# The last chunk of two layers done tile by tile, third sums released sooner, and the parked residual stream cut into eight pieces

## The chip, the cores and the metric

The kernel runs on one core of a Trainium2 chip. The metric is the device time of one execution in microseconds (us), lower is better. The core has five engines that run side by side, each with its own instruction queue: TensorE (PE: matmuls, with a weight-load part PEld), VectorE (DVE), ScalarE (ACT), GpSimd (POOL) and SyncE (SP), which here only issues DMA transfers. Engines wait for each other through semaphores; transfers run on 16 DMA engines that all queues share.

## The reference

One encoder layer in fp32 over 256 positions of 2048 features. Three sub-layers follow each other; each normalises its input, multiplies it with weights, normalises the result and adds it to the residual stream h:

```python
hn = rms_norm(h, g_mix_pre)
u = hn @ w_in                                   # 2048 x 5120
attn, rec = attention(q, k, v), rglru(xr) * gelu(yg)
mixed = concat(rms_norm(attn), rms_norm(rec)) @ w_out      # 2048 x 2048
h = h + rms_norm(mixed, g_mix_post)
fn = rms_norm(h, g_ffn_pre)
ff = (silu(fn @ w_ffn_gate) * (fn @ w_ffn_up)) @ w_ffn_down  # 2048 x 5632 x 2048
h = h + rms_norm(ff, g_ffn_post)
gate = sigmoid(rms_norm(h, g_ple_pre) @ w_ple_gate)        # 2048 x 2048
h = h + rms_norm(gate * (p @ w_ple_proj), g_ple_post)      # p is 256 wide
```

What matters here are the two seams at which h gets its addition: no matmul of the next sub-layer can start until the last column of `mixed` (or of `ff`) is there, because the norm needs the sum of squares over all 2048 columns.

## The kernel before, in words

**Numbers.** A matmul in fp32 is made of three in a rounded format (fp32r): every operand is split into a high part (a cast on ACT) and the rest (a subtraction on DVE), and hi x hi, lo x hi and hi x lo are summed. A weight tile is 256 rows (two blocks of 128) by 512 columns, 512 KB: SP loads it into `wr`, ACT casts `wh` from it (L699), DVE subtracts `wl` (L715), and PE runs twelve matmuls with it: two blocks, two row tiles of 128 positions (`acc0`, `acc1`), three products (L753 to L755 in `products`).

**Chunks.** The output columns are taken 512 at a time. A chunk is such a quarter of 2048 columns, with its two accumulators `acc0` and `acc1`; its `post` runs when its last weight tile is done. The two tiles' matmuls alternate within each block, so both accumulators are finished almost together.

**The seam.** For the mixing layer the post of a chunk is `Sub.chunk`: ACT sums the squares of each accumulator (`squares`, L1612), DVE multiplies it by the gain into `mg` (L1594). For the channel layer DVE first adds what earlier groups left (L1582). When all four chunks are done, `next_norm` adds up the squares (L1627), gets 1/rms (a root on ACT, L397, a reciprocal on DVE, L399) and updates h in place, in pieces of 256 columns per tile (L1652). Blocks of h are transposed by PE (L343) and split into `hT_hi` (ACT, L330) and `hT_lo` (DVE, L332) for the next sub-layer. The last quarter (blocks 12 to 15) is turned in another way: DVE transposes 32x32 pieces, small DMA moves (`mT<-mid`, L362) put them in place, and the split reads `mT`. While the seam lasts, PE does matmuls that don't depend on it: those of the embedding `p @ w_ple_proj` (`embedding(0)`, `embedding(1)`).

**Third sums.** Some pairs of blocks of the channel layer are multiplied by a scheme with seven products for eight. It needs sums of blocks of hT (`sums_of`: L866, L873, then a split on ACT L324 and DVE L326), one set for each pair, and sums of weights (`sum_stream`: L640, L642, L646), which wait for the sums of hT. The third set, `more_sums`, uses blocks 4 and 5 and a buffer that had held `mg`; it starts when every block of hT has been made (`for e in hF.ev`).

**Parking.** `spill_h` writes h (two tiles of 128x2048, 1 MB each) to device memory, so that its place can hold weights (`lower`, `third`) until it is read back at the end of the channel layer. It is planned at the end of `next_norm`, and waits for all blocks of hT.

**Order.** The kernel is written under a planner that simulates the engines' clocks as it emits instructions. Work for the engines is a set of generators (tasks); when an engine is free, the planner picks among the tasks that are ready by time and by a lateness that each carries (`-SOON` brings it forward by 2 us, `LATE` puts it back). The order in which it emits is the order of each queue, and nothing overtakes in a queue.

## Time and profile before

| | |
|---|---|
| Median of 3 runs | 1139.5 us (1138.98 to 1141.05) |
| Profiled execution | 1141.41 us, span 1139.6 |
| PE busy | 1129.5 us, 99% of the span |
| DVE busy | 962.8 us, 84% |
| ACT busy | 741.3 us, 65% |
| POOL busy | 154.8 us, 14% |
| Mean DMA traffic | 237 GB/s |

All times in the profile's rows are us from the start of the span. A row of a timeline gives start, busy time, engine, line of the kernel, operation, output and inputs, and in brackets how long the engine had been idle before and what ended that. `x4` folds four equal instructions in a row. Durations of neighbours overlap a little, so the distance between starts is the better price. A row of waits gives total, number and longest. A row of stretches gives the stretch, its length, the busy time and count of PE, PEld, DVE, ACT and POOL, the granted clock of PE, the DMA share and GB/s. A row of transfers ends with the size of one and its median time from issue to landing. The mixing layer's seam lies around 340 to 362 us, the third sums around 380 to 396, the channel layer's seam around 1030 to 1052.

### The profile page before, as it was taken

The numbers are of one execution on the slowest core, as the hardware profiler recorded it, in microseconds if no ns is written. First come the engines' busy times: TensorE is split into PE (matmuls) and PEld (weight loads), VectorE is DVE, ScalarE is ACT, GpSimd is POOL, SyncE is SP. The second block draws the span as 40 slices with busy tenths as digits, with TensorE's granted clock in tenths as the row PEclk, the third lists the DMA queues.
The fourth block names the chain that finished last, engine by engine and source line by source line (L and its number), as shares of the span: only waits on it lengthen the run. The fifth ranks groups of instructions, "written<-read, shape, count | busy, mean of one in ns | idle before, by whom it ended". The sixth has DMA issues, their size and how long they took to land.

```text
span 1139.6 us, 15226 instructions
## 1 busy us (share of the span) xinstructions
PE 1129.5 (99%) x5140; PEld 937.4 (82%) x5140; DVE 962.8 (84%) x1250; ACT 741.3 (65%) x994; POOL 154.8 (14%) x245
## 2 busy tenths in 40 slices
PE   9999999999999999999999999999999999999997
PEld 7888888888888788888888888888888888888886
DVE  6768787788468899899998889999999988988886
ACT  6776788976447556566566656666656664676674
POOL 0000000000000032132011033141121223100200
PEclk9999999999999999999999999999999999999999
DMA  8867666565786977787887777887888787877863
GB/s 313 300 193 220 170 187 184 166 200 181 212 299 184 317 258 235 233 254 223 271 294 225 249 215 217 254 264 228 275 276 285 226 248 250 290 227 269 263 194 109
DMA packets 110687, 269.54 MB, mean 237 GB/s; under 512 B 36433, under 2 KB 42577, under 8 KB 109201
## 3 DMA queue, kind: packets, MB, share of 16 engines
q1 hardware_dynamic: 95568, 242.60, 63.6%
q0 software_dynamic: 14752, 25.84, 11.3%
q8 instruction: 40, 0.66, 0.2%
q14 instruction: 39, 0.31, 0.1%
q10 hardware_dynamic: 288, 0.14, 0.0%
HBM read 250.70 MB, written 9.44 MB: 228 GB/s over the span
## 4 chain that ended last, share of the span: by engine, by line
PE 96%; DVE 2%; ACT 1%; issue 0%; DMA 0%; SPq 0%; DVEq 0%; POOL 0%; ACTq 0%; POOLq 0%
PE acc L755 23%; PE acc L753 23%; PE acc L754 23%; PE acc L766 7%; PE acc L765 7%; PE acc L764 7%; PE tr L343 1%; DVE wl L715 1%; DMA sq<-ev 0%; PE half L2068 0%; PE acc L2068 0%; PE warm L2254 0%; PE pg L390 0%; PE pg L391 0%; PE pg L392 0%
## 5 line engine op out<-in xcount | busy, mean ns | idle before, releaser
L715 DVE TENSOR_TENSOR wl<-wr,wh 128x1024 fp32r<-128x1024 f32 (+1 forms) x295 | 352.7, 1209 | 78.8 <-ACT wh L699 74.6
L699 ACT CAST wh<-wr 128x1024 fp32r<-128x1024 f32 (+1 forms) x295 | 305.3, 1044 | 145.8 <-PE acc L754 83.4
L753 PE MATMUL acc<-wh,hT_mix_hi 128*128 128x512 f32 x376 | 146.6, 390 | 0.0
L754 PE MATMUL acc<-wh,hT_mix_lo 128*128 128x512 f32 x376 | 146.4, 389 | 0.0
L755 PE MATMUL acc<-wl,hT_mix_hi 128*128 128x512 f32 x376 | 146.3, 389 | 0.0
L699 ACT CAST wh<-ple 128x1024 fp32r<-128x1024 f32 (+1 forms) x75 | 76.1, 1019 | 84.8 <-DVE ple L642 54.6
L362 POOL DMA_DIRECT2D mT<-mid x164 | 97.0, 635 | 232.3 <-DVE mid L352 95.6
L755 PE MATMUL acc<-wl,hT_hi 128*128 128x512 f32 x320 | 124.9, 391 | 0.0
L753 PE MATMUL acc<-wh,hT_hi 128*128 128x512 f32 x316 | 124.6, 394 | 0.0
L754 PE MATMUL acc<-wh,hT_lo 128*128 128x512 f32 x316 | 123.2, 390 | 0.0
L668 POOL DMA_DIRECT2D ple<-in_w_ffn_up x32 | 28.7, 897 | 544.8 <-DVE ple L642 388.5
L715 DVE TENSOR_TENSOR wl<-ple,wh 128x1024 fp32r<-128x1024 f32 (+1 forms) x75 | 87.9, 1177 | 9.5 <-ACT wh L699 9.5
L754 PEld LDWEIGHTS acc<-wh,hT_mix_lo 128*128 128x128 f32 x376 | 70.6, 188 | 14.9 <-DVE hT_mix_lo L332 0.3
L755 PEld LDWEIGHTS acc<-wl,hT_mix_hi 128*128 128x128 f32 x376 | 70.6, 188 | 14.8
L753 PEld LDWEIGHTS acc<-wh,hT_mix_hi 128*128 128x128 f32 x376 | 70.6, 188 | 14.7 <-ACT hT_mix_hi L330 0.2
L755 PEld LDWEIGHTS acc<-wl,hT_hi 128*128 128x128 f32 x320 | 60.1, 188 | 13.8 <-DVE wl L715 0.9
L754 PEld LDWEIGHTS acc<-wh,hT_lo 128*128 128x128 f32 x316 | 59.4, 188 | 11.7
L753 PEld LDWEIGHTS acc<-wh,hT_hi 128*128 128x128 f32 x316 | 59.4, 188 | 11.3
L715 DVE TENSOR_TENSOR wl<-lower,wh 128x1024 fp32r<-128x1024 f32 x35 | 42.3, 1213 | 2.4 <-ACT wh L699 2.4
L699 ACT CAST wh<-lower 128x1024 fp32r<-128x1024 f32 x35 | 36.6, 1051 | 10.5 <-PE acc L754 6.7
L753 PE MATMUL acc<-wh,hT_ffn_hi 128*128 128x512 f32 x96 | 37.7, 393 | 0.2 <-ACT hT_ffn_hi L330 0.2
L715 DVE TENSOR_TENSOR wl<-third,wh 128x1024 fp32r<-128x1024 f32 x29 | 35.4, 1220 | 2.6 <-ACT wh L699 2.4
(477 smaller groups left out, 2559.6 us busy)
## 6 DMA issues: line engine op xcount, KB each, us to landing
wr<-in_w_in SPq DMA_DIRECT2D x77, 512.0 KB, 4.5
wr<-in_w_ffn_gate SPq DMA_DIRECT2D x70, 512.0 KB, 5.5
wr<-in_w_ffn_down SPq DMA_DIRECT2D x54, 512.0 KB, 6.0
wr<-in_w_ffn_up SPq DMA_DIRECT2D x50, 512.0 KB, 4.9
wr<-in_w_out SPq DMA_DIRECT2D x32, 512.0 KB, 4.3
wr<-in_w_ple_gate SPq DMA_DIRECT2D x30, 512.0 KB, 5.0
lower<-in_w_ffn_up SPq DMA_DIRECT2D x27, 512.0 KB, 5.7
third<-in_w_ffn_gate SPq DMA_DIRECT2D x18, 512.0 KB, 5.5
```

Source lines behind the costliest of these rows:

```text
L343: nc.tensor.transpose(tr[:, b, t * P : (t + 1) * P], e[:, t, sl], ident)
L362: (nc.gpsimd if i in pool else nc.sync).dma_start(dst[32 * j : 32 * j + 32, :, :, i, :], src[32 * i : 32 * i + 32, :, :, j, :],)
L668: nc.gpsimd.dma_start(dst, src, accum_op=ALU.add)
L699: nc.scalar.copy(his[i][:, 0 : src.shape[1], :] if n == 2 else his[i][:, j, :], src)
L715: nc.vector.tensor_tensor(out=los[i][:, m, :], in0=src, in1=f32(his[i][:, m, :]), op=ALU.subtract)
L753: nc.tensor.matmul(accs[t], hi[:, sl], his[i][:, j, :], start=st, stop=False, **group)
L754: nc.tensor.matmul(accs[t], lo[:, sl], his[i][:, j, :], start=False, stop=False, **group)
L755: nc.tensor.matmul(accs[t], hi[:, sl], los[i][:, j, :], start=False, stop=sp, **group)
L764: nc.tensor.matmul(dst, x[0], wh, start=start, stop=False, skip_group_check=seeded)
L765: nc.tensor.matmul(dst, x[1], wh, start=False, stop=False, skip_group_check=seeded)
L766: nc.tensor.matmul(dst, x[0], wl, start=False, stop=stop, skip_group_check=seeded)
```

## The change

Three things change.

1. **Tile by tile.** For the last chunk of the mixing layer (`ch[3]`) and of the channel layer (`last_down`), the last weight tile's twelve matmuls are reordered: six for `acc0`, then six for `acc1`. Each accumulator gets its own post (`Sub.tile`), added when its six are done, with lateness `-SOON` for its squares, adds and gains. `next_norm` gets `-SOON` too. The weight buffer is given back after the second tile (`hold`).
2. **Third sums.** `more_sums` waits for `ev_merged`, which is done when h has been updated, and not for all blocks of hT; its own blocks 4 and 5 are waited for in `sums_of`.
3. **Parking.** `spill_h(c)` writes one column quarter, two pieces of 128x512 (256 KB), and is planned after quarter c's updates, so eight transfers take the place of two.

The planner then orders anew. Three places of the order follow. First VectorE at the seam of the mixing layer: `acc_2998` and `acc_2999` are the last chunk's accumulators, `h_2905` and `h_2906` the two tiles of h. Before:

```order
L1594 TENSOR_TENSOR mg_2908<-acc_2999,gain_g_mix_post 128x512
L1627 TENSOR_REDUCE tot_mix<-ss_mix 128x2
L399 RECIPROCAL ro_mix<-rt_mix 128x2
L715 TENSOR_TENSOR wl<-wr,wh 128x1024
L1652 SCALAR_TENSOR_TENSOR h_2905<-mg_2907,ro_mix,h_2905 128x256
...
L1652 SCALAR_TENSOR_TENSOR h_2905<-mg_2907,ro_mix,h_2905 128x256
L332 SCALAR_TENSOR_TENSOR hT_mix_lo<-tr,vec,hT_mix_hi 128x256
L1652 SCALAR_TENSOR_TENSOR h_2906<-mg_2908,ro_mix,h_2906 128x256
L332 SCALAR_TENSOR_TENSOR hT_mix_lo<-tr,vec,hT_mix_hi 128x256
```

After:

```order
L1633 TENSOR_TENSOR mg_2908<-acc_2999,gain_g_mix_post 128x512
L1660 TENSOR_REDUCE tot_mix<-ss_mix 128x2
L400 RECIPROCAL ro_mix<-rt_mix 128x2
L1687 SCALAR_TENSOR_TENSOR h_2905<-mg_2907,ro_mix,h_2905 128x256
...
L333 SCALAR_TENSOR_TENSOR hT_mix_lo<-tr,vec,hT_mix_hi 128x256
L1687 SCALAR_TENSOR_TENSOR h_2905<-mg_2907,ro_mix,h_2905 128x256
L1687 SCALAR_TENSOR_TENSOR h_2906<-mg_2908,ro_mix,h_2906 128x256
L1687 SCALAR_TENSOR_TENSOR h_2905<-mg_2907,ro_mix,h_2905 128x256
L1687 SCALAR_TENSOR_TENSOR h_2906<-mg_2908,ro_mix,h_2906 128x256
L716 TENSOR_TENSOR wl<-wr,wh 128x1024
L333 SCALAR_TENSOR_TENSOR hT_mix_lo<-tr,vec,hT_mix_hi 128x256 x3
```

The weight split that stood between the reciprocal and the first update of h now stands behind twelve updates and one `hT_lo`, and the other `hT_lo` stand behind it. On PE the embedding's second half now lies between two groups of eight transposes. On SP the first four pieces of h now stand ahead of a weight load that used to be third behind the seam:

```order
L612 DMA wr<-in_w_ffn_gate 128x1024
L1751 DMA h_spill<-h_2905 128x512
L1751 DMA h_spill<-h_2906 128x512
L1751 DMA h_spill<-h_2905 128x512
L1751 DMA h_spill<-h_2906 128x512
L612 DMA wr<-in_w_ffn_up 128x1024
L1764 DMA ple_spill<-ple 256x1x1024
```

Second VectorE at the third sums, where `s` is the third set and `hT_mix_lo<-mT` are the splits of the last quarter. Before:

```order
L332 SCALAR_TENSOR_TENSOR hT_mix_lo<-mT,vec,hT_mix_hi 128x256 x4
L866 TENSOR_TENSOR ple<-hT_mix_hi,hT_mix_lo 128x256 x2
L873 TENSOR_TENSOR ple<-ple 128x128 x4
L326 TENSOR_TENSOR s<-ple,s 128x512
L640 TENSOR_TENSOR ple<-wr 128x512
```

After:

```order
L333 SCALAR_TENSOR_TENSOR hT_mix_lo<-mT,vec,hT_mix_hi 128x256
L327 TENSOR_TENSOR sf<-ple,sf 128x512
L867 TENSOR_TENSOR ple<-hT_mix_hi,hT_mix_lo 128x256
L716 TENSOR_TENSOR wl<-wr,wh 128x1024
L333 SCALAR_TENSOR_TENSOR hT_mix_lo<-mT,vec,hT_mix_hi 128x256
L716 TENSOR_TENSOR wl<-wr,wh 128x1024
L333 SCALAR_TENSOR_TENSOR hT_mix_lo<-mT,vec,hT_mix_hi 128x256 x2
L867 TENSOR_TENSOR ple<-hT_mix_hi,hT_mix_lo 128x256
L874 TENSOR_TENSOR ple<-ple 128x128 x4
L327 TENSOR_TENSOR s<-ple,s 128x512
L641 TENSOR_TENSOR ple<-wr 128x512
```

The four splits of the last quarter no longer stand in one piece ahead of the sums: one and the first L867 moved ahead of two weight splits. On SP the last two of that stretch's gate and up loads now follow each other directly, without mT moves between them. Third VectorE at the seam of the channel layer, where `mg_8413` and `mg_8475` (`mg_8419` and `mg_8481` in the change) are the two tiles' sums. Before:

```order
L715 TENSOR_TENSOR wl<-wr,wh 128x1024 x2
L1582 TENSOR_TENSOR mg_8413<-acc_8570,mg_8413 128x512
L1582 TENSOR_TENSOR mg_8475<-acc_8571,mg_8475 128x512
L1594 TENSOR_TENSOR mg_8413<-mg_8413,gain_g_ffn_post 128x512
L1627 TENSOR_REDUCE tot_ffn<-ss_ffn 128x2
L1594 TENSOR_TENSOR mg_8475<-mg_8475,gain_g_ffn_post 128x512
L399 RECIPROCAL ro_ffn<-rt_ffn 128x2
```

After:

```order
L716 TENSOR_TENSOR wl<-wr,wh 128x1024
L1626 TENSOR_TENSOR mg_8419<-acc_8576,mg_8419 128x512
L716 TENSOR_TENSOR wl<-wr,wh 128x1024
L1633 TENSOR_TENSOR mg_8419<-mg_8419,gain_g_ffn_post 128x512
L1626 TENSOR_TENSOR mg_8481<-acc_8577,mg_8481 128x512
L716 TENSOR_TENSOR wl<-wr,wh 128x1024
L1633 TENSOR_TENSOR mg_8481<-mg_8481,gain_g_ffn_post 128x512
L1660 TENSOR_REDUCE tot_ffn<-ss_ffn 128x2
L400 RECIPROCAL ro_ffn<-rt_ffn 128x2
```

Two weight splits that stood ahead of the adds or behind the first updates now stand between the adds and the gains, ahead of the reduce. The split that stood between the third and the fourth update (not shown) is now behind all sixteen.

The diff, cut to its core:

```diff
@@ run_seg
-        for n, (_, kx) in enumerate(ks):
+        m = len(ks) - (BY_TILE if last and chunk.tile_post else 0)
+        for n, (_, kx) in enumerate(ks[:m]):
             i = i0 + n
...
-        if last:
+        for t in range(NT) if m < len(ks) else ():
+            for n in range(m, len(ks)):
+                products(i0 + n, ks[n][1], lhs, chunk.accs, [t], False, n == len(ks) - 1,
+                         seeded=bool(chunk.made), hold=t < NT - 1)
+            plan.add(chunk.tile_post(chunk, t), plan.clk["pe"] + plan.SEM, chunk.late)
+            plan.run()
+        if last and m == len(ks):
@@ more_sums
-        for e in hF.ev:
-            yield e
+        yield ev_merged
@@ class Sub
+        def tile(self, c, ch, t, add):
+            sl = slice(c * N, (c + 1) * N)
+            mg = t2["mg"]
+            yield ev_gain[self.name]
+            src = ch.accs[t]
+            if add:
+                yield ev_sums_back
+                yield dve(N)
+                nc.vector.tensor_tensor(out=mg[:, t, sl], in0=src, in1=mg[:, t, sl], op=ALU.add)
+                src = mg[:, t, sl]
+            squared = Event()
+            plan.add(self.squares(c, t, src, squared), plan.now, ch.late)
+            if add:
+                yield squared
+            yield dve(N)
+            nc.vector.tensor_tensor(out=mg[:, t, sl], in0=src, in1=t2["gain"][:, sl], op=ALU.mult)
+            yield squared
+            done(self.tiles[t])
...
@@ next_norm
         for c in range(4):
             if c > 1:
                 yield nxt.ev[4 * c - 8]
+            if c and sub is mix:
+                plan.add(spill_h(c - 1), plan.now)
...
+        if sub is mix:
+            done(ev_merged)
+        if sub is mix:
+            plan.add(spill_h(3), plan.now)
...
-        if sub is mix:
-            plan.add(spill_h(), plan.now)
@@ spill_h
-    def spill_h():
-        for e in hF.ev:
-            yield e
+    def spill_h(c):
+        sl = slice(c * N, (c + 1) * N)
         for t, ev in enumerate((ev_spilled, ev_all_spilled)):
-            yield dma(1024)
-            nc.sync.dma_start(spill[t], t2["h"].tiles[t])
-            done(ev)
-            plan.now += 40.0 if t == 0 else 0.0
+            yield dma(256)
+            nc.sync.dma_start(spill[t][:, sl], t2["h"].tiles[t][:, sl])
+            if c == 3:
+                done(ev)
@@ layers
+    def by_tile_post(sub, c, add, after):
+        def post(ch, t):
+            if t == NT - 1:
+                plan.add(after(), plan.now, -SOON if sub is mix else -SOON)
+            yield from sub.tile(c, ch, t, add)
+        return post
...
+    ch[3].tile_post = by_tile_post(mix, 3, False, after_mix)
+    ch[3].late = -SOON
...
+    last_down = groups[-1].chunks[1][0]
+    last_down.tile_post = by_tile_post(ffn, 3, True, after_ffn)
+    last_down.late = -SOON
```

More of the change, by code (lines that the diff above doesn't have):

```diff
@@ L90 @@
 AHEAD = 5
+BY_TILE = 1
 ISSUE = 160
@@ L433, in __init__ @@
             self.post, self.before, self.late, self.slot = post, before, late, slot
-            self.accs, self.made = None, None
+            self.accs, self.made, self.tile_post = None, None, None
             self.ready, self.free = Event(), Event()
@@ L728, in layer, with products @@
     MM4 = 0.9
-    def products(i, kx, lhs, accs, ts, start, stop, *after, seeded=False):
+    def products(i, kx, lhs, accs, ts, start, stop, *after, seeded=False, hold=False):
         group = {"skip_group_check": seeded}
@@ L756, in products @@
             at_pe[0] = max(at_pe[0], i)
-            if j:
+            if j and not hold:
                 free_w(i)
@@ L896, in fourth_sums @@
         yield from sums_of(hF, 6, pair[:, 0, :], pair[:, 1, :])
-    ev_unmerged = Event()
+    ev_unmerged, ev_merged = Event(), Event()
     def free_w(i):
@@ L1564, in __init__ @@
             self.sums = [[Event() for _ in range(NT)] for _ in range(4)]
+            self.tiles = [Event() for _ in range(NT)]
             ev_gain[name] = Event()
@@ L1607, in chunk @@
             done(self.chunks[c])
+        def tile(self, c, ch, t, add):
[17 more added lines that the diff above has]
+            if t == NT - 1:
+                for e in self.tiles:
+                    yield e
+                ch.release()
+                done(self.chunks[c])
         def squares(self, c, t, src, ev):
@@ L1780, in sub_post @@
         return post
+    def by_tile_post(sub, c, add, after):
+        def post(ch, t):
+            if t == NT - 1:
+                plan.add(after(), plan.now, -SOON if sub is mix else -SOON)
+            yield from sub.tile(c, ch, t, add)
+        return post
     def after_mix():
```

## The prediction

> **What bounds the kernel now.** I read the page's busy table and chain first, then the waits of TensorE, then the timelines of TensorE (PE), VectorE (DVE), ScalarE (ACT) and SyncE's queue (SP) at the three places that the change touches, and last the table of stretches and the transfers.
>
> ```profile
> PE 1129.5 (99%) x5140; PEld 937.4 (82%) x5140; DVE 962.8 (84%) x1250; ACT 741.3 (65%) x994; POOL 154.8 (14%) x245
> PE 96%; DVE 2%; ACT 1%; issue 0%; DMA 0%; SPq 0%; DVEq 0%; POOL 0%; ACTq 0%; POOLq 0%
> PE acc L766 <- DVE wl L715: 0.5, 1, 0.5
> PE acc L753 <- ACT hT_ffn_hi L330: 0.2, 1, 0.2
> 385.66 0.39 PE L754 MATMUL acc<-wh,hT_mix_lo 128*128 128x512 f32 x1
> 388.38 0.39 PE L754 MATMUL acc<-wh,hT_mix_lo 128*128 128x512 f32 x1
> ```
>
> PE is busy 99% of the span and carries 96% of the chain: the count of matmuls sets the time, and the change removes none. Of the waits, only these two, 0.7 us, lie where the change acts. But matmul ends are modelled, so a short wait hides inside a "busy" record; starts tell more. From 385.66 to 388.38 lie twelve matmuls, so one takes 2.72 / 12 = 0.227 us. Losses are found by holding starts against that pace. So the change can win the small gaps at three places and no more. The span is 1139.6 in an execution of 1141.41 us; the median of the timed runs is 1139.5, 1.9 lower. I work out a difference and take it from the median. A measurement of this kernel tells about 0.2%, 2.3 us, from no change.
>
> **Third sums.** The largest gap.
>
> ```profile
> 388.61 0.39 PE L755 MATMUL acc<-wl,hT_mix_hi 128*128 128x512 f32 x1
> 390.20 0.50 PE L766 MATMUL acc<-wl,at_hi 128*128 128x512 f32 x1 [0.53 <-DVE wl L715]
> 393.68 0.50 PE L766 MATMUL acc<-w,sf 128*128 128x512 f32 x1
> 396.12 0.39 PE L753 MATMUL acc<-wh,hT_mix_hi 128*128 128x512 f32 x1
> 380.48 1.23 DVE L715 TENSOR_TENSOR wl<-wr,wh 128x1024 fp32r<-128x1024 f32 x1 [1.29 <-ACT wh L699]
> 381.62 1.67 DVE L332 SCALAR_TENSOR_TENSOR hT_mix_lo<-mT,vec,hT_mix_hi 128x256 fp32r<-128x256 f32 x4
> 383.21 0.76 DVE L866 TENSOR_TENSOR ple<-hT_mix_hi,hT_mix_lo 128x256 f32<-128x256 f32 x2
> 384.00 1.02 DVE L873 TENSOR_TENSOR ple<-ple 128x128 f32<-128x128 f32 x4
> 385.70 0.69 DVE L326 TENSOR_TENSOR s<-ple,s 128x512 fp32r<-128x512 f32 x1 [0.69 <-ACT s L324]
> 386.31 0.68 DVE L640 TENSOR_TENSOR ple<-wr 128x512 f32<-128x512 f32 x1
> 379.39 1.05 ACT L699 CAST wh<-wr 128x1024 fp32r<-128x1024 f32 x1 [1.28 <-DMA wr<-in_w_ffn_up]
> 372.28 1.24 SPq L362 DMA_DIRECT2D mT<-mid  x2
> 373.62 0.54 SPq L611 DMA_DIRECT2D wr<-in_w_ffn_up  x1
> ```
>
> Between 388.61 and 396.12 PE starts 25 intervals: 25 x 0.227 = 5.67 of 7.51 us, so 1.84 us are lost to three weight splits of DVE in a row. The third serves the matmul at 393.68, fifteen after 388.61, due at 388.61 + 15 x 0.227 = 392.01: 1.67 late. DVE works without a gap from 386.31 on, so that stall goes if L640 starts by 386.31 - 1.67 = 384.64.
>
> What delays L640? The third sums wait until all sixteen blocks of hT are there, though they read blocks 4 and 5; the last four come by the mT moves and their splits (381.62 to 383.21). With `ev_merged` those splits no longer stand ahead of L866, and the order puts two of four earlier. The load issued at 373.62, behind two mT moves, landed just before ACT's cast of 379.39, which waited for it: about 5.7 later. In the new order it follows the gate load directly, about 1.3 sooner: 372.3 + 5.7 = 378.0. Then: cast 378.1 + 1.05 - 0.1 overlap, split to 380.3, two L333 0.8 (381.1), one L867 0.4 (381.5), L874 1.0 (382.5), ACT's cast 0.65, last L327 0.65: 383.85, 0.8 inside the limit. So the term is **-1.8**. Its bounds: 0 (the load no sooner and later transfers worse) and -1.84. If the load alone stays where it was, L640 is 1.3 later, 385.15, and 0.5 of the stall remains.
>
> **End of the mixing layer.**
>
> ```profile
> 343.55 0.69 DVE L1594 TENSOR_TENSOR mg<-acc,gain_g_mix_post 128x512 f32<-128x512 f32 x1 [1.33 <-ACT junk L1612]
> 344.15 0.15 DVE L1627 TENSOR_REDUCE tot_mix<-ss_mix 128x2 f32<-128x8 f32 x1
> 344.78 1.23 DVE L715 TENSOR_TENSOR wl<-wr,wh 128x1024 fp32r<-128x1024 f32 x1
> 345.93 2.85 DVE L1652 SCALAR_TENSOR_TENSOR h<-mg,ro_mix,h 128x256 f32<-128x256 f32 x7
> 347.44 1.54 PE L343 MATMUL tr<-ident,h 128*128 128x128 f32 x12
> 353.65 0.39 PE L754 MATMUL acc<-wh,hT_mix_lo 128*128 128x512 f32 x1
> 361.63 0.39 PE L753 MATMUL acc<-wh,hT_mix_hi 128*128 128x512 f32 x1
> ```
>
> With its twelve matmuls tile by tile, the second gain no longer waits for both squares, and ACT's root no longer stands behind a cast: I put the reduce at 343.7, the first update at 344.5, against 345.93. Of the 1.4 us, 1.15 is only the split L715, which now stands behind twelve updates: 344.5 + 8 x 0.395 (2.85 / 7, less the overlap of neighbours) + one hT_lo 0.4 + 4 x 0.395 = 349.6, the split to 350.75, the second hT_lo to 351.15. The embedding's matmuls keep PE until 347.44 as before, wherever the transposes stand among them; sixteen transposes, 1.6, and the six matmuls of the first block, 1.36, bring it to 350.4, and the second matmul of the next block wants that hT_lo at 350.7: 0.4 lost. A later one, behind four updates and two turns, I find about 0.3 late, a rougher estimate. Today's loss: 347.44 to 353.65 is 6.21 us for 24 transposes, about 0.10 each, and 13 matmuls, 2.95: 0.65 to 0.86 by the transposes' price. I expect 0.9 instead, PE through its fourth weight tile near 361.8 for 361.6: **+0.2**. Bounds: -0.65 (all of today's loss goes) and +0.8 (both hT_lo a split later).
>
> **End of the channel layer.**
>
> ```profile
> 1032.94 2.35 DVE L715 TENSOR_TENSOR wl<-wr,wh 128x1024 fp32r<-128x1024 f32 x2
> 1035.22 1.28 DVE L1582 TENSOR_TENSOR mg<-acc,mg 128x512 f32<-128x512 f32 x2
> 1037.68 0.16 DVE L1627 TENSOR_REDUCE tot_ffn<-ss_ffn 128x2 f32<-128x8 f32 x1
> 1038.64 1.28 DVE L1652 SCALAR_TENSOR_TENSOR h<-mg,ro_ffn,h 128x256 f32<-128x256 f32 x3
> 1040.78 1.27 PE L343 MATMUL tr<-ident,h 128*128 128x128 f32 x8
> 1049.94 0.39 PE L753 MATMUL acc<-wh,hT_ffn_hi 128*128 128x512 f32 x1
> ```
>
> Here the order takes away what the tiles give. Both L715 ran before the adds; now one stands behind the first add and one behind the second. From an add at 1034.2 (six matmuls earlier): add 0.6, split 1.15, gain 0.6, add 0.6, split 1.15, gain 0.6, reduce 0.1: 1039.0 against 1037.68, and the updates start near 1039.65, 1.0 later. The split that followed three updates is postponed, so the fourth update ends as before, 1041.3, but an hT_lo now behind two splits comes late: sixteen updates (6.3), four hT_lo (1.6), two turns (1.2, priced as gains of the same width) and two splits (2.3) lie ahead of it, so it ends at 1051.5, about 0.4 after PE wants it; another 0.1 goes at the first transposes. Today's loss from 1040.78 to 1049.94 is 9.16 - 24 x 0.227 - 24 x 0.10 = 1.3. I add **+0.5**; bounds -0.5 and +1.0 (the whole later start).
>
> **The eight pieces.**
>
> ```profile
> 342.00:349.00 7.00, 7.00 (x38) 5.74 (x36) 5.16 (x13) 5.85 (x12) 0.00 (x0) 1.00 0.48 152
> 381.00:389.00 8.00, 8.00 (x37) 6.35 (x35) 7.21 (x17) 2.84 (x6) 0.00 (x0) 1.00 1.03 409
> 346.07 0.33 SPq L611 DMA_DIRECT2D wr<-in_w_ffn_up  x1
> 382.59 0.90 SPq L1715 DMA_DIRECT2D h_spill<-h  x2
> wr<-in_w_ffn_up SPq DMA_DIRECT2D x50, 512.0 KB, 4.9
> ```
>
> The bytes are the same, 2 MB. Half move from a stretch whose DMA share is 1.03 to one of 0.48. But the first four now stand on SP ahead of the load of 346.07, and each waits for updates of its quarter, until 347.7 for the fourth. Eight issues for two, at 0.45 us each, put the load behind four at about 349.5; its buffer's earlier split ends at 350.75 by then, so it goes at 350.8. I find its weights split near 367.2 against 367.7 when PE wants them (two tiles of 12 matmuls and two more after 361.8: 26 x 0.227 = 5.9). The cover is half a us; term **0**, from -0.2 (the busy stretch eased) to the price in rival D.
>
> The sum: -1.8 + 0.2 + 0.5 + 0 = -1.1, 1138.4 for the median.
>
> **The rivals.** A is that forecast. B: the third sums are freed and the earlier updates win the restart too: -1.8, -0.65, and nothing at the channel layer: -2.45, 1137.0. For it speaks the 1.4 us; against, that the split is only postponed. C: the transfers near 380, at a share of 1.03, land no sooner, so the third sums' stall stays: 0 + 0.2 + 0.5 = +0.7, 1140.2; with half the stall, 1139.3. For it, DMA binds the cast of 379.39 today; against, that load is issued sooner by two moves.
>
> D, the slower side: SP pays each piece through to its landing.
>
> ```profile
> mT<-mid SPq DMA_DIRECT2D x44, 32.0 KB, 3.3
> out<-h SPq DMA_DIRECT2D x4, 256.0 KB, 2.7
> 361.88 0.62 ACT L1666 ACTIVATE junk<-h 128x512 f32<-128x512 f32 x1
> ```
>
> At 3.3 us each from 346.1 the load behind four would issue at 359.3, land 4.9 later at 364.2, and its cast end at 365.2; eight squares at 0.62 and two hT_hi at 0.4 (5.8) stand on ACT ahead of the next cast and split (2.1): 373.1 where PE wants 367.7, a stall of 5.4: -1.1 + 5.4 = +4.3, 1143.8. At 2.7 each it is 2.4 less, 1141.4. The stall begins with a load issued after 353.9; the change is a loss from 355.0. Against it: SP issues mT<-mid two in 1.24 us at 372.28, far under 3.3 each.
>
> Beside it, the Trainium skill, page "DMA: Bandwidth & Descriptors", section "Anatomy of one DMA — SWDGE (gpsimd) path", gives each DMA about 2.0 us fixed beside its bytes, mostly the receipt of its end. Six more DMAs would by that, as an estimate from the page and if paid in turn, cost 12 us of queue. The row of two moves in 1.24 us says that the issuing queue does not pay it here; the page's own account, a delay of completion, agrees with that.
>
> **How the numbers follow.** A 0.55, B 0.20, C 0.16, D 0.09. Range 1136.4 to 1141.0: below, B and 0.6 more, the channel layer's lower bound; above, C and most of D's milder price. A and C lie within 2.28 us of before; half of B's spread lies beyond it, and 0.03 of A's: faster 0.13. D is slower: 0.09. Same: 0.78.
>
> **What would show it.** Right: no L766 wait near 390 and DVE's L641 (the L640 of before) by 384.6; first update of the mixing layer near 344.5, of the channel layer near 1039.7; the load behind the pieces issued near 350.8. Wrong: PE waits for hT_lo longer than a split at either restart, or a wait for a weight split between 365 and 373, which is D; or L641 still near 386, which is C.

## The result, and the profile after

| us | before | change |
|---|---|---|
| median of 16 runs | 1139.55 (1138.98 to 1141.08) | 1141.9 (1140.52 to 1142.57) |
| change over before, 95% interval | | 1.0018 (1.0011 to 1.0025) |
| profiled execution | 1141.41 | 1142.47 |
| its span | 1139.6 | 1140.7 |

The change costs 2.35 us where a gain of 1.1 was forecast, and ends 0.9 above the range. The interval leaves out "no change", but not by much: it reaches from 0.11% to 0.25% slower. The sixteen times of the change fall into two groups, seven from 1140.52 to 1141.16 and eight from 1142.12 to 1142.57, with one between; its median lies between them, and the profiled execution is one of the upper group. Of the sixteen of before, four lie at 1140.46 or higher.

The busy table and the chain in the profile after:

```profile
PE 1129.9 (99%) x5140; PEld 937.0 (82%) x5140; DVE 963.2 (84%) x1250; ACT 741.1 (65%) x994; POOL 154.8 (14%) x245
PE 90%; DVE 4%; DMA 2%; ACT 2%; issue 1%; POOL 0%; SPq 0%; DVEq 0%; ACTq 0%; POOLq 0%
```

And TensorE's waits (engine and line, what it waited for, us in total, times, longest):

```profile
PE acc L756 <- DVE w L716: 0.5, 1, 0.5
PE acc L755 <- DVE hT_ffn_lo L333: 0.4, 1, 0.4
PE acc L766 <- DVE pTl L327: 0.2, 1, 0.2
PE acc L755 <- DVE hT_mix_lo L333: 0.2, 1, 0.2
```

The 5140 matmuls are the same. The wait of the third sums near 390 (0.5 before) is gone. Four short ones stand in its place: near 474, at the restart of the channel layer, at the third sums of the last layer, and at the restart of the mixing layer.

**Third sums.** Timelines of PE, DVE and ACT after:

```profile
388.56 0.39 PE L756 MATMUL acc<-wl,hT_mix_hi 128*128 128x512 f32 x1
392.03 0.50 PE L767 MATMUL acc<-w,sf 128*128 128x512 f32 x1
394.46 0.39 PE L754 MATMUL acc<-wh,hT_mix_hi 128*128 128x512 f32 x1
384.67 0.68 DVE L641 TENSOR_TENSOR ple<-wr 128x512 f32<-128x512 f32 x1
378.71 1.04 ACT L700 CAST wh<-wr 128x1024 fp32r<-128x1024 f32 x1
```

From 388.56 to 394.46 lie 25 intervals: 5.90 - 5.67 = 0.23 us lost, for 1.84 before. L641 starts at 384.67 (forecast: by 384.6), and the cast no longer waits for a load. The step went as forecast, and the kernel is slower all the same.

**The two restarts** (the places at the seams where PE takes up the next sub-layer). DVE, PE and SP after:

```profile
344.10 3.26 DVE L1687 SCALAR_TENSOR_TENSOR h<-mg,ro_mix,h 128x256 f32<-128x256 f32 x8
349.24 1.22 DVE L716 TENSOR_TENSOR wl<-wr,wh 128x1024 fp32r<-128x1024 f32 x1
350.91 0.50 PE L755 MATMUL acc<-wh,hT_mix_lo 128*128 128x512 f32 x1 [0.18 <-DVE hT_mix_lo L333]
345.40 2.38 SPq L1751 DMA_DIRECT2D h_spill<-h  x4
350.53 0.33 SPq L612 DMA_DIRECT2D wr<-in_w_ffn_up  x1
1033.97 1.22 DVE L716 TENSOR_TENSOR wl<-wr,wh 128x1024 fp32r<-128x1024 f32 x1
1036.31 1.22 DVE L716 TENSOR_TENSOR wl<-wr,wh 128x1024 fp32r<-128x1024 f32 x1
1038.77 3.26 DVE L1687 SCALAR_TENSOR_TENSOR h<-mg,ro_ffn,h 128x256 f32<-128x256 f32 x8
1041.94 0.48 DVE L333 SCALAR_TENSOR_TENSOR hT_ffn_lo<-tr,vec,hT_ffn_hi 128x256 fp32r<-128x256 f32 x1
1041.59 0.47 PE L754 MATMUL acc<-wh,hT_ffn_hi 128*128 128x512 f32 x1
1042.47 0.50 PE L755 MATMUL acc<-wh,hT_ffn_lo 128*128 128x512 f32 x1 [0.41 <-DVE hT_ffn_lo L333]
1050.16 0.39 PE L754 MATMUL acc<-wh,hT_ffn_hi 128*128 128x512 f32 x1
1050.67 0.50 PE L755 MATMUL acc<-wh,hT_ffn_lo 128*128 128x512 f32 x1
```

The updates begin at 344.10 and 1038.77 (forecast 344.5 and 1039.65), the split behind twelve mixing updates runs at 349.24 (forecast 349.6), and the load behind the pieces is issued at 350.53 (forecast 350.8). The forecasts count on the clock of the first profile of before; this execution is 0.3 ahead of that one near 345 and 0.8 near 1030 (the table below), so they read 344.2, 1038.8, 349.3 and 350.5 here. At both places PE waits once, briefly, for an hT_lo. Every sign that the prediction named for being right has come, within about 0.1 us, and none of those for being wrong: the signs told where things happen, and not what they are worth.

### The profile page after: what moved, and what is told of

It reads as the page before. It is cut to its first block, busy times and chain, and to the rows that moved or that the text cites. A ratio compares the mean times of both kernels' runs of the same rounds, so it can differ in the third digit from the quotient of the medians.

```text
span 1140.7 us, 15230 instructions
## 1 busy us (share of the span) xinstructions
PE 1129.9 (99%) x5140; PEld 937.0 (82%) x5140; DVE 963.2 (84%) x1250; ACT 741.1 (65%) x994; POOL 154.8 (14%) x245
## 4 chain that ended last, share of the span: by engine, by line
PE 90%; DVE 4%; DMA 2%; ACT 2%; issue 1%; POOL 0%; SPq 0%; DVEq 0%; ACTq 0%; POOLq 0%
PE acc L756 22%; PE acc L755 22%; PE acc L754 22%; PE acc L766 7%; PE acc L767 7%; PE acc L765 7%; DVE wl L716 1%; DMA mT<-mid 1%; DVE h L1687 1%; PE tr L344 1%; DMA sq<-ev 0%; PE half L2116 0%; PE acc L2116 0%; DMA wr<-in_w_in 0%; PE warm L2302 0%
## 5 line engine op out<-in xcount | busy, mean ns | idle before, releaser
L755 PE MATMUL acc<-wh,hT_ffn_lo 128*128 128x512 f32 x96 | 37.6, 392 | 0.5 <-DVE hT_ffn_lo L333 0.4
```

Source lines behind the costliest of these rows:

```text
L755: nc.tensor.matmul(accs[t], lo[:, sl], his[i][:, j, :], start=False, stop=False, **group)
```

## Where each execution loses time

To see more than waits, the start of every matmul in one profile was held against the start of the same matmul (by its place in PE's order) in another: the lag. What the lag gains between two places is what that stretch lost. In the table everything is held against one later profile of the kernel before (an execution of 1140.23, called the second profile; the one that the prediction read is the first), so its own losses enter every row with the opposite sign. "Mix", "channel": the restarts; "3rd": the third sums near 390; "last": the third sums of the last layer; "end": from the last rows of matmuls to the end of the span, good to 0.1, since it uses spans rounded to that. The stretches 495 to 1000 and 1095 to 1128 hold less than 0.02 in every row. "Prio" is the planner's priority for the tiles' work and the norm behind it, which the experiments explain.

```
us, lag gained in a stretch         us  to 30  -300   mix   3rd  -495 chann. -1083  last   end
before, first profile          1141.41  -0.33 +0.68  0.00 +1.26 +0.01 -0.02 -0.41  0.00 +0.02
the change                     1142.47  -0.71 +0.78 +0.23 -0.37 +0.87 +0.55 -0.12 +0.49 +0.58
the change, profile a          1140.83  -0.58 +0.22 +0.24 -0.55  0.00 +0.54 -0.28 +0.54 +0.47
the change, profile b          1141.50  -0.51 -0.05 +0.23 -0.09  0.00 +0.56 +0.15 +0.52 +0.49
the change, profile c          1141.53  +0.57 +0.35 +0.27 -0.60  0.00 +0.54 -0.42 +0.12 +0.58
no channel tiles               1139.42  -0.47 -0.08 +0.24 -0.57  0.00  0.00 -0.41  0.00 +0.49
no early sums                  1142.56  -0.51 -0.01 +0.25 +1.42 -0.01 +0.66 -0.32 +0.58 +0.34
no mix tiles                   1141.78  -0.18 +0.83  0.00 -0.12  0.00 +0.54 -0.26 +0.54 +0.25
no pieces                      1140.81  -0.02 -0.08 +0.26 +0.11  0.00 +0.55 -0.41 +0.20 -0.01
channel tiles only             1140.60  -0.68 -0.03 -0.01 -0.20  0.00 +0.52 +0.07 +0.58 +0.16
early sums only                1139.00  -0.38 +0.22 -0.04 -0.60 +0.01 -0.02 -0.39  0.00  0.00
early sums only, again         1140.39  -0.30 +0.19 -0.01 -0.10 +0.35 -0.03 +0.06  0.00 +0.04
mix tiles only                 1141.04  -0.54 +0.51 +0.21 +1.09  0.00 -0.02 -0.42  0.00 +0.07
pieces only                    1140.68  -0.63 +0.59 -0.01 +0.59  0.00 -0.02 -0.41  0.00 +0.40
pieces only, from GpSimd       1141.07  -0.06 +0.77 +0.02 +0.44  0.00  0.00 -0.41  0.00 +0.14
channel tiles only, no prio    1140.39  +0.32 +0.34  0.00 -0.07  0.00 -0.29 -0.17  0.00 +0.07
mix tiles only, no prio        1139.47  -0.31 -0.09 -0.12 +0.19  0.00 -0.02 -0.42  0.00 +0.07
the change, no prio            1140.50  -0.14 +0.40 -0.12 -0.60  0.00 -0.28 +0.82  0.00 +0.22
the change, no prio, no pieces 1140.69  -0.17 +0.83 -0.09 -0.60  0.00 -0.28 +0.68  0.00 +0.13
```

Three columns depend on the kernel alone: mix, channel, and (with few exceptions) last. The others vary between executions of one kernel: the first 300 us alone, ahead of all that the diff touches, spread over 1.6 us (lags of -0.71 to +0.92 by then), over 1.5 us within the four profiles of the change.

## The experiments

The theory tested first was the prediction's: third sums -1.8, mix +0.2, channel +0.5, pieces 0. Its rival was that parts which the prediction put at nothing carry the loss.

### One part of the change undone

**Without the channel layer's tiles.** The channel layer goes back to one post for both tiles.

```diff
-    last_down = groups[-1].chunks[1][0]
-    last_down.tile_post = by_tile_post(ffn, 3, True, after_ffn)
-    last_down.late = -SOON
```

> The change without its tile-by-tile chunk at the end of the channel layer; the rest stays. Theory (the channel layer's reordering costs about 1.35 us: 0.55 at the seam, 0.8 at the last layer's third sums, whose four small subtractions now stand one by one between weight splits): 1.3 to 1.9 us less than the change, 1140.0 to 1140.6, about 0.5 over the kernel before, and no PE wait for pTl. Rival (the eight pieces or the busier transfers cost it): it stays at the change's 1141.9, within 0.5.

Measured 1140.79 (1139.42 to 1141.6, 11 runs; before beside it 1139.64), ratio 1.0008 (0.9999 to 1.0017). The tiles cost 1.1 in the change: 0.55 at the restart and 0.12 to 0.54 at the last layer's third sums, which go with them (both columns are 0.00 here). The rest isn't placed. The theory had asked for a little more, 1.3 to 1.9. The intervals of the two kernels taken together leave such a difference uncertain by some 1.3 us, here and in the next three runs, so none of the four prices is clear of nothing by time alone.

**Without the early third sums.**

```diff
-        yield ev_merged
+        for e in hF.ev:
+            yield e
```

> The change with the third sums waiting for all blocks again. Theory (the early sums win 1.5 us near 390 and the new order of the later groups gives 0.8 back near 474): 0.7 us more than the change, 1142.6; the stall of 1.8 near 390 returns, the lag of 0.8 near 474 is gone. Rival (the early sums are lost on net, since the planner's later order costs more than they win): at or under the change's 1141.9.

Measured 1142.56 (1140.69 to 1143.7, 9 runs; before 1139.64), ratio 1.0025 (1.0015 to 1.0035). The theory had 1142.6. So the early sums are worth 0.66 inside the change, not 1.8. In its profile the loss near 390 is back, 1.42 above the second profile. A row of PE near 390 and the first L643 of DVE's timeline:

```profile
389.77 0.50 PE L767 MATMUL acc<-wl,at_hi 128*128 128x512 f32 x1 [0.53 <-DVE wl L716]
386.60 0.69 DVE L643 TENSOR_TENSOR ple<-ple,lower 128x512 f32<-128x512 f32 x1 [1.34 <-DMA lower<-in_w_ffn_up]
```

Here DVE itself waits 1.34 for a transfer.

**Without the mixing layer's tiles.**

```diff
-    ch[3].tile_post = by_tile_post(mix, 3, False, after_mix)
-    ch[3].late = -SOON
```

> The change without its tile-by-tile chunk at the end of the mixing layer. Theory (that edit costs 0.1 us at its seam): 1141.8, within 0.3 of the change. Rival (the seam's new order delays the last quarter of hT and with it the sums): 0.5 or more under the change.

Measured 1140.69 (1140.26 to 1141.78, 11 runs; before 1139.64), ratio 1.0011 (1.0002 to 1.002): the tiles cost 1.2 in the change, as the rival had it, of which their restart shows 0.23 to 0.27.

**Without the pieces.** The two spills of 1 MB as before, planned again at the end of `next_norm` (the edit is cut to its core).

```diff
-            yield dma(256)
-            nc.sync.dma_start(spill[t][:, sl], t2["h"].tiles[t][:, sl])
+            yield dma(1024)
+            nc.sync.dma_start(spill[t], t2["h"].tiles[t])
...
```

> The change with h parked in two transfers of 1 MB as before. Theory (the pieces are hidden): 1141.9, within 0.3 of the change. Rival (the pieces cost the time, in the queue or at the DMA engines): 1139.5 to 1140.5.

Measured 1141.02 (1139.81 to 1142.74, 11 runs; before 1139.64), ratio 1.0013 (1.0004 to 1.0021): the pieces cost 0.9 in the change, between the two expectations. The four undone parts add up to 1.1 - 0.66 + 1.2 + 0.9 = 2.5, close to the 2.35 of the whole; with 1.3 us of uncertainty on each, the closeness may be chance.

### One part alone

Each of these four is the kernel before with one part of the change; the lines are those shown above or in the diff.

**Channel layer's tiles alone.**

```diff
+    last_down = groups[-1].chunks[1][0]
+    last_down.tile_post = by_tile_post(ffn, 3, True, after_ffn)
+    last_down.late = -SOON
```

> The kernel before with the tile-by-tile chunk at the end of the channel layer alone. Theory: 1.35 us over before (seam 0.55, third sums of the last layer 0.8): 1140.9, with the PE wait for pTl. Rival (the seam's loss is one of the combination only): within 0.4 of before, 1139.1 to 1139.9.

Measured 1140.85 (1140.35 to 1142.13, 11 runs; before 1139.57), ratio 1.0011 (1.0003 to 1.002): +1.3. Its profile shows the same two losses, +0.52 at the restart and +0.58 at the last layer's third sums. The second, on DVE and PE (`mid` are the sums that the last layer's third set is made of, `pTl` the low part of their split):

```profile
1079.67 0.28 DVE L874 TENSOR_TENSOR mid<-mid 128x128 f32<-128x128 f32 x1
1081.01 0.29 DVE L874 TENSOR_TENSOR mid<-mid 128x128 f32<-128x128 f32 x1
1082.35 0.28 DVE L874 TENSOR_TENSOR mid<-mid 128x128 f32<-128x128 f32 x1
1083.68 0.69 DVE L327 TENSOR_TENSOR pTl<-mid,pTh 128x512 fp32r<-128x512 f32 x1
1084.42 0.50 PE L766 MATMUL acc<-wh,pTl 128*128 128x512 f32 x1 [0.24 <-DVE pTl L327]
```

Against the kernel before, second profile:

```profile
1078.87 0.28 DVE L873 TENSOR_TENSOR mid<-mid 128x128 f32<-128x128 f32 x1
1079.07 1.22 DVE L715 TENSOR_TENSOR wl<-wr,wh 128x1024 fp32r<-128x1024 f32 x1
1080.20 0.68 DVE L326 TENSOR_TENSOR pTl<-mid,pTh 128x512 fp32r<-128x512 f32 x1
1084.35 0.39 PE L765 MATMUL acc<-wh,pTl 128*128 128x512 f32 x1
```

The small subtractions that make up `mid` ended at 1079.15 before, and `pTl` was ready 3.5 us ahead of its matmul. With the tiles' work ahead they come one by one, a weight split of 1.2 us between each two, and `pTl` ends when PE already waits. The same three L874 and L327 stand in the profile of the change at 1081.19 to 1085.20. The prediction did not look at this place, 30 us behind the last thing that the diff touches.

**Early third sums alone.**

```diff
-        for e in hF.ev:
-            yield e
+        yield ev_merged
```

> The kernel before with the early third sums alone. Theory: -1.5 near 390, +0.8 near 474: 0.7 us under before, 1138.9. Rival (the lag near 474 comes of the pieces or of the mixing layer's tiles, not of the sums): -1.5, 1138.0. Third: the 0.8 is only half of what comes back, no change, 1139.5.

Measured 1139.14 (1138.59 to 1140.17, 11 runs; before 1139.57), ratio 0.9996 (0.9987 to 1.0005). Timed once more later:

> The kernel before with the early third sums alone, timed again beside the kernel before. Theory (an ordinary execution of the kernel before loses 0.6 near 390 and this edit takes it away): 0.3 to 0.7 under before. Rival (what is won near 390 is lost at later orders): within 0.2 of before.

Measured 1139.78 (1138.42 to 1140.44, 11 runs; before 1139.5), ratio 1.0000 (0.9991 to 1.0009). So alone this part moves the time by -0.4 and +0.3, which is nothing that can be measured. The loss near 390 is gone in the first of the two profiles; in the second 0.5 of it is left, and 0.35 is lost near 474. DVE in the first, with L641 at 383.35, is in good time:

```profile
382.74 0.69 DVE L327 TENSOR_TENSOR s<-ple,s 128x512 fp32r<-128x512 f32 x1 [0.29 <-ACT s L325]
383.35 0.69 DVE L641 TENSOR_TENSOR ple<-wr 128x512 f32<-128x512 f32 x1
```

**Mixing layer's tiles alone.**

```diff
+    ch[3].tile_post = by_tile_post(mix, 3, False, after_mix)
+    ch[3].late = -SOON
```

> The kernel before with the tile-by-tile chunk at the end of the mixing layer alone. Theory: +0.1, 1139.6, within 0.3. Rival (the hT_lo behind a split costs as priced, but the sums, still late, get later): +0.5 or more.

Measured 1141.04 (1139.25 to 1141.5, 11 runs; before 1139.57), ratio 1.001 (1.0001 to 1.0019): +1.5, of which the restart shows 0.21. The profile has 1.09 more than the second profile near 390; the cast there waits for its load again:

```profile
379.87 1.05 ACT L700 CAST wh<-wr 128x1024 fp32r<-128x1024 f32 x1 [0.67 <-DMA wr<-in_w_ffn_up]
385.99 0.68 DVE L641 TENSOR_TENSOR ple<-wr 128x512 f32<-128x512 f32 x1
```

**Pieces alone.**

```diff
+            if c and sub is mix:
+                plan.add(spill_h(c - 1), plan.now)
```

> The kernel before with h parked in eight pieces alone. Theory: no change, within 0.3 of 1139.5. Rival (pieces in line pay to their landing): +1 or more.

Measured 1140.5 (1139.39 to 1141.91, 11 runs; before 1139.57), ratio 1.0006 (0.9997 to 1.0015). The 0.9 is again more than the forecast's 0 and just under the rival's 1, with an interval that just holds no change (a ratio of 1).

### What in the parts costs

**Pieces from GpSimd.** If SP's queue, standing behind the pieces' waits, is what costs, moving them to another queue gives the time back; if their bytes or their landing cost, it doesn't.

```diff
-            yield dma(256)
-            nc.sync.dma_start(spill[t][:, sl], t2["h"].tiles[t][:, sl])
+            yield ("pool", COST["move"], None, None, None)
+            nc.gpsimd.dma_start(spill[t][:, sl], t2["h"].tiles[t][:, sl])
```

> The kernel before with h parked in eight pieces, issued by GpSimd instead of SyncE; nothing else. Theory (the pieces cost 0.9 us because they stand in SyncE's queue among the loads and moves, each of which waits for the landing of the transfer eight issues earlier): within 0.3 of before, 1139.3 to 1139.9. Rival (the bytes come at a bad time for the loads at the DMA engines): as with the pieces on SyncE, 1140.2 to 1140.8.

Measured 1140.52 (1139.5 to 1141.56, 11 runs; before 1139.52), ratio 1.0008 (1.0 to 1.0017): about the same 1.0, in the rival's range. The queue theory is not borne out, though the interval reaches from nothing to 1.9 us. GpSimd's rows, and then the transfers' group (KB each, median us from issue to landing):

```profile
348.34 1.81 POOL L1752 DMA_DIRECT2D h_spill<-h  x3 [346.12 <-DVE h L1688]
350.44 0.55 POOL L1752 DMA_DIRECT2D h_spill<-h  x1 [0.29 <-DVE h L1688]
357.48 0.54 POOL L1752 DMA_DIRECT2D h_spill<-h  x1 [0.25 <-DVE h L1688]
```

```profile
h_spill<-h POOLq DMA_DIRECT2D x8, 256.0 KB, 4.0
```

Here the last piece is issued at 357.48, far ahead of the busy stretch near 380, and still the profile has a loss of 0.44 above the second profile near 390. With the kernel before at 0 and at +1.26 in that column, a single profile of 0.44 proves nothing; the column "end" does say something, and is taken up below. Three issues take 1.81 us and a landing 4.0. The Trainium skill, page "DMA: Bandwidth & Descriptors", section "Anatomy of one DMA — SWDGE (gpsimd) path", puts about 2.0 us fixed on each such DMA, most of it a delay of completion; the rows agree that the issuing queue doesn't pay it, at 0.6 us an issue. (The prediction took that figure for SP's pieces; the section is about GpSimd's.)

**Tiles without priority.** The change adds the tiles' work, and the norm behind it, to the planner with a lateness of `-SOON`, 2 us ahead of its turn. Theory: that priority, rather than the tiles, makes one unbroken run of updates and pushes the splits and hT_lo behind it. Each of the two edits is made to the kernel with the tiles of one layer alone, and takes the priority from the posts and from the norm behind them (`after`) together; which of the two counts was not separated.

```diff
-                plan.add(after(), plan.now, -SOON if sub is mix else -SOON)
+                plan.add(after(), plan.now, -SOON if sub is mix else 0.0)
...
-    last_down.late = -SOON
+    last_down.late = 0.0
```

> The kernel before with the tile-by-tile chunk at the end of the channel layer alone, its tasks without the lateness of -2 us: the splits still stand between the adds and the gains, but updates of h and hT_lo alternate again, as before. Theory (the splits ahead of the reduce cost it, and the last layer's third sums stay between splits): 1140.4 to 1141.0, like the run with the priority. Rival (the unbroken run of updates ahead of the hT_lo costs it): 1139.3 to 1139.9.

Measured 1140.11 (1139.45 to 1143.86, 11 runs; before 1139.52), ratio 1.0007 (0.9998 to 1.0016), between the two expectations. The profile is clearer than the time: the restart gains 0.29 instead of losing 0.52, and the loss at the last third sums is gone. DVE at the restart:

```profile
1038.55 2.07 DVE L1686 SCALAR_TENSOR_TENSOR h<-mg,ro_ffn,h 128x256 f32<-128x256 f32 x5
1040.90 0.48 DVE L333 SCALAR_TENSOR_TENSOR hT_ffn_lo<-tr,vec,hT_ffn_hi 128x256 fp32r<-128x256 f32 x1 [0.28 <-ACT hT_ffn_hi L331]
1041.31 0.48 DVE L1686 SCALAR_TENSOR_TENSOR h<-mg,ro_ffn,h 128x256 f32<-128x256 f32 x1
```

The splits still stand between the adds and the gains, and the first update starts as late as in the change: 1038.55 and 1038.77, or 1037.96 and 1037.97 when the lag of 0.59 and 0.80 that each has by then is taken off (the second profile of before has 1037.01). But five updates instead of eight stand ahead of the first hT_lo, which starts at 1040.90 instead of 1041.94, without the lags 0.83 earlier; the restart is 0.84 better.

```diff
-                plan.add(after(), plan.now, -SOON if sub is mix else -SOON)
+                plan.add(after(), plan.now, 0.0 if sub is mix else -SOON)
...
-    ch[3].late = -SOON
+    ch[3].late = 0.0
```

> The kernel before with the tile-by-tile chunk at the end of the mixing layer alone, its tasks without the lateness of -2 us: the weight split stands behind eleven updates, and updates and hT_lo alternate from there. Theory (the seam itself is even, and the 1.3 us come from the moves and loads behind it being ordered anew, so that the ninth load lands too late for the third sums): still 0.8 to 1.5 over before, 1140.4 to 1141.0, with the stall near 390. Rival (the priority makes the loss): within 0.3 of before.

Measured 1139.92 (1139.47 to 1141.99, 11 runs; before 1139.52), ratio 1.0005 (0.9996 to 1.0014). The 0.4 is just outside the rival's 0.3 and well under the theory's 0.8. The mixing restart gains 0.12 instead of losing 0.21.

### The same kernels profiled again

**The kernel before**, unchanged, and **the change**, unchanged, three times.

> The kernel before, one more look at its profile. Theory (the stall near 390 is there in the slower of its executions alone, when one move in SyncE's queue waits about 2 us for a load's landing): with a time under 1140.2 the 25 intervals from 388.6 lose at most 0.7 us and SyncE's wait for a load's landing is under 0.7; with a time over 1140.8 they lose 1.5 or more. Rival (the stall is always there): 1.8 lost at any time.

> The change, a second look. Theory (the change's slower executions differ from its faster ones by a late turn near 474, where a move of mT lands late and a split on VectorE waits): with a time under 1141.3 PE loses less than 0.2 between 470 and 486; with a time over 1142 it loses 0.7 or more there. Rival (the slower ones lose it somewhere else, at the start or the end): no loss near 474 at any time.

> The change, a third look, as the second: under 1141.3 less than 0.2 lost between 470 and 486, over 1142 0.7 or more; the rival has no loss there at any time. In every look the seam of the channel layer costs 0.5 to 0.7 and the last layer's third sums 0.2 to 0.6 against the kernel before.

> The change, a fourth look, as the second: under 1141.3 less than 0.2 lost between 470 and 486, over 1142 0.7 or more; the rival has no loss there at any time.

The second profile of the kernel before took 1140.23, just over the 1140.2 of its theory; the three of the change took 1140.83, 1141.5 and 1141.53. The second profile settles the main question, whether every execution of the kernel before loses the 1.84. PE, DVE and ACT in it:

```profile
388.25 0.39 PE L755 MATMUL acc<-wl,hT_mix_hi 128*128 128x512 f32 x1
390.39 0.50 PE L766 MATMUL acc<-wl,hT_mix_hi 128*128 128x512 f32 x1
392.13 0.50 PE L766 MATMUL acc<-w,sf 128*128 128x512 f32 x1
394.53 0.39 PE L753 MATMUL acc<-wh,hT_mix_hi 128*128 128x512 f32 x1
384.77 0.68 DVE L640 TENSOR_TENSOR ple<-wr 128x512 f32<-128x512 f32 x1
377.85 1.06 ACT L699 CAST wh<-wr 128x1024 fp32r<-128x1024 f32 x1 [0.45 <-PE acc L755]
```

Twenty-five intervals in 394.53 - 388.25 = 6.28 us lose 0.61, against 1.84 in the first profile of the same kernel. The cast that waited 1.28 for its load then doesn't wait for one here, and L640 starts at 384.77 instead of 386.31. In the first profile a move on SP, too, had waited longer for a load. SP's transfers take eight semaphores in turn, so that an issue waits for the landing of the transfer eight before it; the load issued at 363.98 landed after 7.01 us, that of 363.62 in the second profile after 6.39. SP's waits in the first profile, then in the second:

```profile
SPq L362 <- DMA wr<-in_w_ffn_up: 2.0, 1, 2.0
```

```profile
SPq L362 <- DMA wr<-in_w_ffn_up: 0.6, 1, 0.6
```

The kernels that have the order of before at this place lose 0.39 and 0.54 (channel tiles only, with and without priority); the four profiles of the change lose 0.23, 0.06, 0.51 and nothing. So an ordinary execution has some 0.5 there, and the change takes 0.3 of it. That the first profile was no ordinary one the times show as well: of 143 timed executions of the kernel before, one took longer than its 1141.41.

The loss of 0.87 near 474 in the first profile of the change is in none of the other three. The one other profile with a loss there is "early sums only, again", at 0.35. With the early sums, GpSimd issues the mT moves for a split (`mid0l`, near 466) some 3 us later, the last near 461 for 458, and VectorE has nothing left to do ahead of that split: it stands idle for 3.09 us in the first profile of the change and 2.58 in the other, and for 1.57 to 2.21 in the nine profiles with early sums that lose nothing; without the early sums it doesn't wait there. So the early sums open a new place where a late landing shows. Whether it makes the upper group of the change's times isn't decided: none of the three further profiles fell into that group.

### Without priority, the whole change

The edit sets both `late` to 0.0, and with them the priority of the work that follows the last tile.

```diff
-                plan.add(after(), plan.now, -SOON if sub is mix else -SOON)
+                plan.add(after(), plan.now, 0.0 if sub is mix else 0.0)
...
-    ch[3].late = -SOON
+    ch[3].late = 0.0
...
-    last_down.late = -SOON
+    last_down.late = 0.0
```

> The change with its tile-by-tile tasks and the norms at plain priority; early sums and pieces on SyncE stay. Theory (the priority's unbroken runs of updates cost 0.24 at the mixing layer's seam, 0.54 at the channel layer's and 0.5 at the last sums; the pieces cost 0.5 at the end of the program): 1.2 to 1.6 under the change, 1140.3 to 1140.7, and after the last output's issue 0.4 to 0.5 us more to the end of the span than the kernel before. Rival (the splits between adds and gains cost it, at any priority): 1141.4 to 1142.

Measured 1140.5 (1139.14 to 1142.54, 11 runs; before 1139.67), ratio 1.0004 (0.9996 to 1.0013). That is 1.4 less than the change, as this theory has it; the end of the program, for which it had 0.4 to 0.5, is 0.2 later. Both restarts gain now, 0.12 and 0.28, but between 1070 and 1083 it loses 0.82 more than the second profile, and 1.2 more than the -0.41 of most profiles without these tiles. There PE waits for a weight split, which neither the change nor the first profile of before shows. Its waits, and the row of the timeline:

```profile
PE acc L767 <- DVE wl L716: 0.9, 1, 0.9
```

```profile
1077.70 0.50 PE L767 MATMUL acc<-wl,hT_ffn_hi 128*128 128x512 f32 x1 [0.91 <-DVE wl L716]
```

**And without the pieces.** The edit is that of the run without the pieces, together with the one above.

> The same with h parked in two transfers as before: early sums and tile-by-tile chunks at plain priority. Theory: 0.3 near 390, 0.1 and 0.3 at the seams, won against the kernel before: 1138.7 to 1139.2, the end of the span as in the kernel before. Rival (each edit's order gives back elsewhere what it wins): 1139.4 to 1140.2.

Measured 1140.55 (1139.25 to 1142.79, 11 runs; before 1139.67), ratio 1.0006 (0.9997 to 1.0015). The theory that the gains at the restarts would now show as a time below before falls; the time is above the rival's range too. They are handed back between 1070 and 1083 as in the run before it, 0.68 more than in the second profile, with the same wait:

```profile
PE acc L767 <- DVE wl L716: 0.8, 1, 0.8
```

The pieces' price may not be a constant: 0.9 in the change and alone, nothing here (1140.5 with them, 1140.55 without), each uncertain by more than a microsecond. No version tried is measurably faster than the kernel before.

**The end of the program.** One thing stands out over all profiles. From PE's last stretch to the end of the span, the nine profiles with the pieces on SP lose 0.22 to 0.58; the ten others in the table, the pieces from GpSimd among them, -0.01 to 0.16 (second profile 0). In the change and in the kernel before, second profile:

```profile
1134.26 1.16 PE L2203 MATMUL final<-mg,diag 128*128 128x256 f32 x2 [2.47 <-ACT diag L2201]
```

```profile
1132.53 0.70 PE L2155 MATMUL final<-mg,diag 128*128 128x256 f32 x2 [2.46 <-ACT diag L2153]
```

The spans end 1140.7 - 1134.26 = 6.44 and 1138.4 - 1132.53 = 5.87 us later. The longer pair of matmuls, 1.16 for 0.70, is no part of it: the part of the output that comes from it lands 4.19 after the pair's start, and SP's last part of the output at 5.00, which is 4.92 in the second profile. The rest lies behind that landing: 1.42 us in the change, 0.97 in the second profile. SP ends the program with nine waits in a fixed order, each for two semaphores, among them the eight that its transfers take in turn. Six more transfers put that last part on another of the eight. In the second profile its landing releases the eighth of the nine waits, in the change the sixth, and the waits behind it still have to pass.

So it is in all ten profiles with eight pieces: the sixth wait, and 1.09 to 1.43 us after the last landing. (GpSimd's pieces are among them: they take two transfers from SP's turn, which comes to the same place as six more in a turn of eight.) In the ten others it is the eighth, and 0.97 to 1.10. In five of the ten, the four of the change among them, one of the waits passes 0.3 later than in the rest; what holds it the traces don't show. The last landing, too, is later with the pieces on SP, 4.96 to 5.13 for 4.90 to 4.94. This is read from the traces; no run varied the number of transfers alone.

## Why the prediction was wrong

**Third sums, -1.8: the step that failed.** Its mechanism was right. The sums come earlier, L641 starts at 384.67 where 384.6 was forecast, the load no longer delays the cast, and the wait is gone. The size was wrong, because the step read its 1.84 from the only profiled execution, which was 1.9 us above the median, and then took the difference off the median. The second profile shows where most of those 1.9 us lay: between the two profiles the third sums differ by 1.26. The term took out time that the median does not contain. By the profiles it is worth 0.3; by time it gains 0.66 inside the change (undone), and alone it gained 0.4 and lost 0.3. This one step makes 1.1 to 1.5 of the 3.5 us between forecast and result.

**End of the mixing layer, +0.2: right.** All eight profiles with the mixing tiles at priority show +0.21 to +0.27, with the updates at 344.10 and the wait for the hT_lo behind the split, as the step had it.

**End of the channel layer, +0.5: right in size, and half right in cause.** +0.52 to +0.66 in all eight profiles with these tiles at priority. The step put it down to the splits between the adds, which make the updates late. They do start 1.0 later, but without priority they start as late, and the restart gains 0.29. PE loses it at two matmuls. One is where the step had it, at the hT_lo behind two splits: PE starts at 1050.67, 0.51 after the matmul before it (0.23 is the pace), where 0.4 lost was forecast. The other is at the first hT_lo, behind the unbroken run of eight updates: PE starts at 1042.47, 0.88 after the matmul before it, for 0.52 in the second profile of before and in the run without priority. In that run the other is gone too.

**What the sum left out: +0.4 at the last layer's third sums.** The change, 0.49, 0.54, 0.52 and 0.12 in four profiles. The prediction costed the places that the diff touches. The planner, which sets the order for all that follows, moved work 30 us later as well, and that place had no term.

**Pieces, 0: too low.** The cover that the step named held: the load was issued at 350.53, and there is no wait for a weight split between 365 and 373, so rival D did not come. But the pieces cost 0.9 in the change and alone. The end of the program, 0.2 to 0.6, is shown; the rest isn't placed, and without priority no price of theirs was seen.

**The sum of what was seen.** Change against before, by the profiles: third sums -0.3, mix +0.24, near 474 +0.2 (0.87 in one of four), channel +0.55, the stretch to 1083 +0.24 (mean of four -0.17, where seven of the nine profiles without channel tiles have -0.39 to -0.42), last +0.42, end +0.5: +1.85 of 2.35. With the first profile of before counted in, the third sums are -0.65 and the sum +1.5. The remaining half to one us was not found in any single place; three of the four profiles of the change lie below its upper group of times, so what that group loses besides may be missing here. Executions of one kernel differ by as much in their first 300 us.

**The rivals.** A failed by its own first term. D at its milder price gave 1141.4 and came nearest, by accident: the wait that it rests on did not come. C, the third sums not relieved, gave 1140.2 and was nearer than A by accident too: they were relieved, but little stood there to win. B needed early updates to win the restarts; with priority they lost them, and without priority the order gave the gain back 30 us later. The 2.3 us that the prediction took as the least measurable difference was wide: the interval of the change is 0.8 us either way.

## What to carry to other kernels

Before a stall is subtracted from a median, see how far the profiled execution lies above that median: what it has too much is somewhere, and the largest stall behind a transfer is the first place to suspect; a second profile of the same kernel tells. Where a planner sets the order, hold the order of the whole program against the old one, and price the places far behind the edit too. And ask of work that is given priority what it stands ahead of: here the earlier updates were not the fault, but that nothing could come between eight of them.

## What was not expected of the hardware

Executions of one kernel lose time at different places: 1.84 or 0.61 us at the same third sums, 0.87 or nothing near 474, with the same order on each engine; where it was followed up, a transfer had landed later. And the end of a program can depend on how many transfers it made 750 us earlier: with eight pieces for two, SP's last output released the sixth of nine closing waits instead of the eighth, and 1.09 to 1.43 us followed its landing for 0.97 to 1.10.
